# Moving a convolution's norm behind the last attention pair, and regrouping the first head of a recurrent layer

## The chip, the cores and the metric

The kernel runs on one core of one Trainium2 chip. The metric is the device time of one execution in microseconds (us), median of several runs. Engines are named as in the profile: PE is TensorE (matmuls; PEld are its weight loads), DVE is VectorE, ACT is ScalarE, POOL is GpSimd, SP is SyncE, whose queue issues the loads and stores.

## The reference, cut to what matters

One inference step through two layers, for a prompt of 512 tokens and for 8 sample sequences of 4 tokens that share the parameters (544 token columns, two halves of 272). The model width is 1024.

```
layer 0:  h = rms(x, norm_0);  q, k, v, g_att, u_a, u_b, g_conv = split(h @ w_in_0)
          attention of 8 heads (block-sparse over 256-token blocks; two blocks: all of the causal part)
          u = u_a * sigmoid(u_b);  y = depthwise_conv31(u) + b
          y = silu(layernorm(y, ln_g, ln_b))            # the convolution's norm, over 512 channels
          x = x + concat(o_att * silu(g_att), y * silu(g_conv)) @ w_out_0
layer 1:  h = rms(x, norm_1);  q, f, i, g = split(h @ w_in_1), 8 heads of 128
          gated linear recurrence per head, rms per head, gate, output projection, residual
```

Sample sequences attend over 256 cached positions (two pages of keys, two of values each). All in fp32 accuracy.

## The kernel before, in words

Activations lie transposed: channels on partitions, 544 tokens along the free axis in two halves of 272. Every projection goes by output blocks of 128 channels. `wtile` (L127) loads one block of weights (512 KB, by SP), and splits it on ACT (L133) and DVE (L134) into two fp32r parts. `unit` (L137) makes one half of one output block: 24 matmuls of 128x272 (L142 to L144) into a PSUM bank of tag "g". There are three banks "g", two of tag "s" (scores), two of tag "t" (transposes and sums) and one "o" (attention output).

Layer 0 works on head pairs 0 to 3. `prepkq` and `prepvg` project a pair, `attend` (L478) computes its prompt attention in four row blocks of 128 queries: for each of two heads the scores (PE, L484 and L486, bank "s"), the row maximum (DVE, L493), exp (ACT, L496), reciprocal (DVE, L497), scaling (ACT, L498), transposes through a bank "t" (PE by way of L102, copied by ACT, L503), and the product with the values (PE, L508). The convolution's 31 taps run as 30 DVE instructions per channel block (`taps`, L379); those of blocks 2 and 3 stand right ahead of the change.

Then, in the order of the source: the convolution's norm (L539 to L564): for each half, DVE adds the four channel blocks (L544, L546), one all-ones matmul sums over channels (L548, bank "t"), DVE subtracts the mean from four blocks (L551), ACT squares them (L553), DVE adds the squares (L555), a second all-ones matmul sums them (L557, bank "t"), ACT takes the square root (L559) and DVE the reciprocal (L560). Behind it the attention of pair 3, and behind that the four gate blocks of the convolution: eight units (L569), each queued behind the first scores of pair 3, with a tanh (L572) and a product (L573). Then the norm is applied (L580, L581), passed through silu (L583, L584) and multiplied by the gate (L585); the sample attention (scores L606, values L645), with pages loaded into the eight buffers "kn", of which the norm's two sum tiles are two; and the output projection in two halves (L666), with layer 1's statistics (L673 to L681).

In layer 1, `proj` (L732) makes a head's four projections ("jobs": f, q, v and g) in groups; a group's weights are loaded together and its units run job by job, first half, then second half. In the first head the second half of h is not yet normalised, so each second-half unit is multiplied by `r1b` (L768). `scan` (L785) is the recurrence; its steps are interleaved with the next head's projections.

The order of each engine's queue is not written by hand: a planner makes it when the program is built. It goes by the order of emission as priority and by its own estimate of when inputs are ready. `tc.issue_after(x)` adds that what is emitted inside is queued behind x on its engine. At run time each engine takes its queue in order.

Of the kernel before, what the change touches and what calls it, by code (L numbers as in the profile page):

```python
# [14 lines left out]
ALU = mybir.AluOpType  # L15
# [51 lines left out]
def hybrid_step(ctx, tc, xt_in, cache_kt, cache_v, conv_in, hgrn_in, page_table, par_in, k_norm_0,  # L67
# [18 lines left out]
    def bank(tag, cols=512, dt=F32):  # L86
        return pp.tile([128, cols], dt, name=nm(tag), tag=tag, bufs={"g": 3, "s": 2, "t": 2, "o": 1}[tag])
# [90 lines left out]
    with tc.tile_pool(name="l0", bufs=1) as lp:  # L178
# [54 lines left out]
        def scaled(ps, hf, u):  # L233
            e = mk(lp, "rs" if u else "ct", [128, HALF], 2)
            V.tensor_tensor(e, ps, rbc[hf], op=ALU.mult)
            return e
# [140 lines left out]
        def taps(c):  # L377
            for j in range(1, 31):
                V.scalar_tensor_tensor(cy[c][:, :TP], up[c][:, j:j + TP], cw[:, c, j:j + 1], cy[c][:, :TP],  # L379
                                       op0=ALU.mult, op1=ALU.add)  # L380
            G.tensor_scalar(up[c][:, 512:542], up[c][:, 512:542], 0.5, 0.0, op0=ALU.mult, op1=ALU.add)
            SP.dma_start(convp_out[:, c], up[c][:, 512:542])
# [93 lines left out]
            return c, rq, qT, kT, vt, ga  # L476

        def attend(c, rq, qT, kT, vt, ga):  # L478
            po, first = bank("o"), None
            for i in range(4):  # L480
                L = 128 * (i + 1)
                ss = [bank("s"), bank("s")]
                for hh in range(2):
                    sc = PE.matmul(ss[hh][:, :L], qT[:, i * 128:(i + 1) * 128], kT[:, hh, 0:L], start=True, stop=False)  # L484
                for hh in range(2):
                    PE.matmul(ss[hh][:, L - 128:L], identb, causb, start=False, stop=True)  # L486
                first = first or sc
                PTs = []
                for hh in range(2):
                    rqc = rq[:, 2 * i + hh:2 * i + hh + 1]  # L490
                    s = ss[hh]
                    mx = mk(lp, "mx", [128, 4], 4)
                    V.tensor_reduce(mx[:, 0:1], s[:, :L], axis=AX.X, op=ALU.max, negate=True)  # L493
                    A.activation(mx[:, 1:2], mx[:, 0:1], AF.Copy, scale=rqc)
                    P = mk(lp, "PP", [128, 512], 3)
                    A.activation(P[:, :L], s[:, :L], AF.Exp, bias=mx[:, 1:2], scale=rqc, accum_out=mx[:, 2:3])  # L496
                    V.reciprocal(mx[:, 3:4], mx[:, 2:3])  # L497
                    A.activation(P[:, :L], P[:, :L], AF.Copy, scale=mx[:, 3:4])  # L498
                    pT = bank("t")
                    for j in range(i + 1):  # L500
                        transpose(pT[:, j * 128:(j + 1) * 128], P[:, j * 128:(j + 1) * 128], 128)
                    PT = mk(lp, "PT", [128, 512], 3)
                    A.activation(PT[:, :L], pT[:, :L], AF.Copy)  # L503
                    PTs.append(PT)
                for j in range(i + 1):
                    for hh in range(2):
                        r = slice(64 * hh, 64 * hh + 64)
                        PE.matmul(po[r, i * 128:(i + 1) * 128], vt[:, j, r],  # L508
                                  PTs[hh][:, j * 128:(j + 1) * 128], start=(j == 0), stop=(j == i),
                                  tile_position=(0, 64 * hh))  # L510
            mh, ml = mtile(("h", c)), mtile(("l", c))
            V.scalar_tensor_tensor(ga[:, :TP], po, 0.5, ga[:, :TP], op0=ALU.mult, op1=ALU.mult)
            split(mh[:, :TP], ml[:, :TP], ga[:, :TP])
            return first

        def convout():
            for i in range(2):
# [17 lines left out]
        p3 = prepvg(*p3)  # L535
        taps(2)
        taps(3)
        rss = []
        at_ = [mk(lp, "kn", [128, T], 8) for _ in range(2)]  # L539
        accs = [[t[:, HC[hf]] for hf in range(2)] for t in at_]  # L540
        for hf in range(2):
            hs = HC[hf]
            acc = accs[0][hf]
            V.tensor_tensor(acc, cy[0][:, hs], cy[1][:, hs], op=ALU.add)  # L544
            for c in range(2, 4):
                V.tensor_tensor(acc, acc, cy[c][:, hs], op=ALU.add)  # L546
            pm = bank("t", HALF)
            PE.matmul(pm, ones, acc, start=True, stop=True)  # L548
            acc = accs[1][hf]
            for c in range(4):  # L550
                V.scalar_tensor_tensor(cy[c][:, hs], pm, -1.0 / 512, cy[c][:, hs], op0=ALU.mult, op1=ALU.add)  # L551
                sq = mk(lp, "ct", [128, HALF], 2) if c else acc
                A.activation(sq, cy[c][:, hs], AF.Square)  # L553
                if c:
                    V.tensor_tensor(acc, acc, sq, op=ALU.add)  # L555
            pq = bank("t", HALF)
            PE.matmul(pq, ones, acc, start=True, stop=True)  # L557
            rs = mk(lp, "rs", [128, HALF], 2)
            A.activation(rs, pq, AF.Sqrt, scale=1.0 / 512, bias=eps)  # L559
            V.reciprocal(rs, rs)  # L560
            rss.append(rs)
        pin = attend(*p3)
        gc = []
        for c in range(4):  # L564
            w = wtile(w_in_0, 3072 + c * 128)
            g2 = up[c]
            for hf in range(2):
                with tc.issue_after(pin.ins):
                    ps = unit(w, h, hf)  # L569
                ps = scaled(ps, 1, 0) if hf else ps  # L570
                tg = mk(lp, "tb", [128, HALF], 3)
                A.activation(tg, ps, AF.Tanh, scale=0.5)  # L572
                V.scalar_tensor_tensor(g2[:, HC[hf]], tg, 1.0, ps, op0=ALU.add, op1=ALU.mult)  # L573
            gc.append(g2)

        for c in range(4):
            tgs = []
            for hf in range(2):
# [107 lines left out]
    with tc.tile_pool(name="l1", bufs=1) as lp:  # L686
# [45 lines left out]
        def proj(hd):  # L732
            f, kk, qq = mk(lp, "f", [128, T], 2), mk(lp, "kk", [128, T], 2), mk(lp, "qq", [128, TP], 2)
            gg, vT = mtile(("gg", hd), F32), mtile(("vT", hd), F32)

            def ep_f(ps, hs):
                A.activation(f[:, hs], ps, AF.Sigmoid)  # L737

            qx = mk(lp, "qx", [128, T // 32, 80], 2)

            def ep_q(ps, hs):
                sg = mk(lp, "sg", [128, HALF], 4)
                A.activation(sg, ps, AF.Sigmoid)
                o = hs.start
                for a, b in ((0, 256), (256, 272)) if o == 0 else ((0, 16), (16, 272)):
                    n = max(1, (b - a) // 32)
                    t0 = (o + a) % 32
                    i0 = (o + a) // 32
                    V.tensor_tensor(qx[:, i0:i0 + n, t0:t0 + (b - a) // n], sg[:, a:b].rearrange("p (n t) -> p n t", n=n),
                                    ps[:, a:b].rearrange("p (n t) -> p n t", n=n), op=ALU.mult)  # L750

            def ep_g(ps, hs):
                sg = mk(lp, "sg", [128, HALF], 4)
                A.activation(sg, ps, AF.Sigmoid)
                V.tensor_tensor(gg[:, hs], sg, ps, op=ALU.mult)

            def ep_v(ps, hs):
                A.activation(vT[:, hs], ps, AF.Copy)

            jobs = ((1024, ep_f), (0, ep_q), (2048, ep_v), (3072, ep_g))  # L760
            for grp in (jobs[:2], jobs[2:]) if hd else ((jobs[2], jobs[0], jobs[1]), jobs[3:]):
                ws = [wtile(w_in_1, col + hd * 128) for col, _ in grp]
                for hf in range(2):
                    for w, (_, ep) in zip(ws, grp):
                        ps = unit(w, h, hf)
                        if hd == 0 and hf:
                            raw = mk(lp, "sg", [128, HALF], 4)
                            V.tensor_tensor(raw, ps, r1b, op=ALU.mult)  # L768
                            ps = raw
                        ep(ps, HC[hf])  # L770
            if hd == 0:
                normed(lp, "n1", r1b, 1)
            V.tensor_scalar(f, f, lbm[:, 5, hd:hd + 1], lbm[:, 4, hd:hd + 1], op0=ALU.mult, op1=ALU.add)
            G.tensor_scalar(kk, f, -1.0, 1.0, op0=ALU.mult, op1=ALU.add)
            vt = mk(lp, "vt", [128, 512], 2)
            pv = bank("t")
            for i in range(4):
                transpose(pv[:, i * 128:(i + 1) * 128], vT[:, i * 128:(i + 1) * 128], 128)
            A.activation(vt, pv, AF.Copy)
            vs = VS[hd % 2]  # L780
            vx = mk(lp, "vx", [128, 128], 2, F32R)
            rep4(vx, vT, (32, 96), 32, vs)
            return f, kk, qx, qq, vt, vs, vx, gg
# [291 lines left out]
```

## Time and profile before

| | |
|---|---|
| median of 3 runs | 661.8 us (661.76 to 663.45) |
| the profiled execution, its own time | 663.44 us |
| its span, first to last instruction | 661.6 us |
| PE busy | 631.2 us (95%) |
| DVE busy | 515.9 us (78%) |
| ACT busy | 367.6 us (56%) |
| POOL busy | 63.7 us (10%) |
| HBM traffic | 105 GB/s over the span |

Times in the profile are counted from the span's start. Busy time of PE is modelled from pipelined matmuls; idle time of PE between two matmuls is time in which none was in flight. The profiled execution was the slowest of the three; what lies around its span is 1.84 us.

### The profile page before, as it was taken

The numbers are of one execution on the slowest core, as the hardware profiler recorded it, in microseconds if no ns is written. First come the engines' busy times: TensorE is split into PE (matmuls) and PEld (weight loads), VectorE is DVE, ScalarE is ACT, GpSimd is POOL, SyncE is SP. The second block draws the span as 40 slices with busy tenths as digits, with TensorE's granted clock in tenths as the row PEclk, the third lists the DMA queues.
The fourth block names the chain that finished last, engine by engine and source line by source line (L and its number), as shares of the span: only waits on it lengthen the run. The fifth ranks groups of instructions, "written<-read, shape, count | busy, mean of one in ns | idle before, by whom it ended". The sixth has DMA issues, their size and how long they took to land.

```text
span 661.6 us, 14877 instructions
## 1 busy us (share of the span) xinstructions
PE 631.2 (95%) x5806; PEld 584.6 (88%) x5806; DVE 515.9 (78%) x1252; ACT 367.6 (56%) x908; POOL 63.7 (10%) x91
## 2 busy tenths in 40 slices
PE   8799999999999959989999899999999999999997
PEld 7699998998996848759999899998999999999997
DVE  6999898888989783846968887787777777776656
ACT  7334486387378475634747463737373737356421
POOL 6100000000100000000001311111111010121000
PEclk9799999999999969989999989999999999999999
DMA  9444321322431231774534134231414141322114
GB/s 297 116 85 108 113 75 41 91 73 64 97 82 65 85 125 33 246 265 149 167 109 158 34 92 135 67 130 38 154 41 143 55 135 62 116 78 92 46 57 148
DMA packets 39016, 70.58 MB, mean 107 GB/s; under 512 B 11938, under 2 KB 20642, under 8 KB 38946
## 3 DMA queue, kind: packets, MB, share of 16 engines
q1 hardware_dynamic: 38946, 69.63, 34.1%
q8 instruction: 46, 0.75, 0.5%
q14 instruction: 24, 0.20, 0.1%
HBM read 59.88 MB, written 9.73 MB: 105 GB/s over the span
## 4 chain that ended last, share of the span: by engine, by line
PE 81%; DVE 8%; ACT 5%; DMA 3%; issue 2%; SPq 1%; DVEq 0%; ACTq 0%
PE g L142 21%; PE g L144 20%; PE g L143 20%; PE t L102 4%; PE o L508 2%; PE s L484 2%; DVE wl L134 2%; ACT wh L133 1%; DMA kn<-in_cache_kt_dram 1%; PE t L933 1%; PE o L946 1%; DMA wr<-in_w_in_dram 1%; PE s L847 1%; PE o L948 1%; DVE tb L167 1%
## 5 line engine op out<-in xcount | busy, mean ns | idle before, releaser
L142 PE MATMUL g<-h,wh 128*128 128x272 f32 x944 | 279.2, 297 | 6.3 <-ACT f L737 3.1
L143 PE MATMUL g<-h,wh 128*128 128x272 f32 x944 | 277.3, 294 | 2.1 <-DVE h L273 2.1
L144 PE MATMUL g<-h,wl 128*128 128x272 f32 x944 | 277.6, 295 | 0.5 <-DVE wl L134 0.5
L142 PEld LDWEIGHTS g<-h,wh 128*128 128x128 f32 x944 | 180.1, 191 | 11.3 <-ACT f L737 3.6
L143 PEld LDWEIGHTS g<-h,wh 128*128 128x128 f32 x944 | 180.0, 191 | 4.8 <-DVE h L273 2.7
L144 PEld LDWEIGHTS g<-h,wl 128*128 128x128 f32 x944 | 180.2, 191 | 3.4 <-issue 2.0
L133 ACT ACTIVATE wh<-wr 128x1024 fp32r<-128x1024 f32 (+4 forms) x90 | 88.0, 980 | 94.2 <-PE g L143 91.3
L134 DVE TENSOR_TENSOR wl<-wr,wh 128x1024 fp32r<-128x1024 f32 (+4 forms) x90 | 101.5, 1129 | 15.0 <-ACT wh L133 14.8
L379 DVE SCALAR_TENSOR_TENSOR m<-m,vecs,m 128x512 f32<-128x512 f32 x120 | 87.4, 740 | 0.7
L142 PE MATMUL g<-m,wh 128*128 128x272 f32 x256 | 75.1, 297 | 0.0
L144 PE MATMUL g<-m,wl 128*128 128x272 f32 x256 | 74.3, 292 | 0.0
L143 PE MATMUL g<-m,wh 128*128 128x272 f32 x240 | 70.0, 293 | 0.0
L142 PEld LDWEIGHTS g<-m,wh 128*128 128x128 f32 x256 | 48.5, 191 | 3.9 <-issue 2.7
L144 PEld LDWEIGHTS g<-m,wl 128*128 128x128 f32 x256 | 48.8, 191 | 1.2 <-issue 1.0
L143 PEld LDWEIGHTS g<-m,wh 128*128 128x128 f32 x240 | 45.8, 191 | 0.1
L910 DVE TENSOR_TENSOR qq<-qq,tot 128x256 f32<-128x256 f32 x24 | 10.0, 415 | 24.9 <-ACT kv L875 22.4
L484 PE MATMUL s<-kz,qT 128*128 128x128 f32 (+3 forms) x64 | 22.8, 447 | 1.4 <-ACT PP L496 1.3
L503 ACT ACTIVATE PT<-t 128x128 f32<-128x128 f32 (+3 forms) x32 | 13.8, 432 | 16.3 <-PE t L102 16.3
L955 POOL TENSOR_TENSOR ve<-vx,cst 128x1024 fp32r<-128x1024 f32 x8 | 15.4, 1930 | 77.1 <-DVE vx L730 63.6
L953 ACT ACTIVATE S<-S,tot 128x128 f32<-128x128 f32 x64 | 20.4, 390 | 1.6 <-PE t L852 1.5
L1014 DVE TENSOR_TENSOR xTall<-g,xTall 128x272 f32<-128x272 f32 x32 | 13.5, 436 | 8.8 <-PE g L144 8.3
L874 ACT ACTIVATE kv<-kk 128x256 f32<-128x256 f32 x16 | 6.6, 411 | 24.5 <-DVE kk L911 20.5
(299 smaller groups left out, 1027.1 us busy)
## 6 DMA issues: line engine op xcount, KB each, us to landing
wr<-in_w_in_dram SPq DMA_DIRECT2D x58, 512.0 KB, 3.7
wr<-in_w_out_dram SPq DMA_DIRECT2D x16, 512.0 KB, 3.6
kn<-in_cache_kt_dram SPq DMA_DIRECT2D x16, 256.0 KB, 4.0
kn<-in_cache_v_dram SPq DMA_DIRECT2D x16, 256.0 KB, 4.4
S<-in_hgrn_dram SPq DMA_DIRECT2D x8, 512.0 KB, 3.6
out_hgrns_dram<-S SPq DMA_DIRECT2D x8, 512.0 KB, 2.6
xTall<-in_xt_dram SPq DMA_DIRECT2D x8, 272.0 KB, 5.5
out_y_dram<-xTall SPq DMA_DIRECT2D x8, 272.0 KB, 2.9
```

What stands on the lines that cost most here:

```text
L102: PE.transpose(out, in_, ident[:np_, :np_])
L133: A.activation(wh, raw, AF.Copy)
L134: V.tensor_tensor(wl, raw, wh, op=ALU.subtract)
L142: PE.matmul(ps, wh[:, k - k0, :], ah, start=(k == k0), stop=False)
L143: PE.matmul(ps, wh[:, k - k0, :], al, start=False, stop=False)
L144: PE.matmul(ps, wl[:, k - k0, :], ah, start=False, stop=(k == k1 - 1))
L379: V.scalar_tensor_tensor(cy[c][:, :TP], up[c][:, j:j + TP], cw[:, c, j:j + 1], cy[c][:, :TP], op0=ALU.mult, op1=ALU.add)
L484: sc = PE.matmul(ss[hh][:, :L], qT[:, i * 128:(i + 1) * 128], kT[:, hh, 0:L], start=True, stop=False)
L503: A.activation(PT[:, :L], pT[:, :L], AF.Copy)
L953: A.activation(S0[:, n], S0[:, n], AF.Copy, scale=tots[:, n:n + 1])
L955: G.tensor_tensor(ve, vx.unsqueeze(1).to_broadcast([128, NS, 128]), exm.unsqueeze(2).to_broadcast([128, NS, 128]), op=ALU.mult)
L1014: V.tensor_tensor(xT[c][:, HC[hf]], ps, xT[c][:, HC[hf]], op=ALU.add)
```

## The change

`attend` returns the last scores matmul of each of its four row blocks instead of that of the first one. The attention of pair 3 is emitted ahead of the norm; so are the gate blocks 0 and 1 (`gates(0)`, `gates(1)`), still queued behind the first row block's scores. Then comes the norm, with two differences: its four sums go to banks "g" instead of "t", and the sum of squares of half 0 is queued behind the third row block's scores, that of half 1 behind the fourth's. `gates(2)` and `gates(3)` follow the norm. In layer 1 the first head's jobs come in the groups (f, q) and (v, g), as in all other heads, instead of (v, f, q) and (g). No arithmetic is added or taken away.

```diff
--- before.py
+++ after.py
@@ -476,7 +476,7 @@
             return c, rq, qT, kT, vt, ga
 
         def attend(c, rq, qT, kT, vt, ga):
-            po, first = bank("o"), None
+            po, firsts = bank("o"), []
             for i in range(4):
                 L = 128 * (i + 1)
                 ss = [bank("s"), bank("s")]
@@ -484,7 +484,7 @@
                     sc = PE.matmul(ss[hh][:, :L], qT[:, i * 128:(i + 1) * 128], kT[:, hh, 0:L], start=True, stop=False)
                 for hh in range(2):
                     PE.matmul(ss[hh][:, L - 128:L], identb, causb, start=False, stop=True)
-                first = first or sc
+                firsts.append(sc)
                 PTs = []
                 for hh in range(2):
                     rqc = rq[:, 2 * i + hh:2 * i + hh + 1]
@@ -511,7 +511,7 @@
             mh, ml = mtile(("h", c)), mtile(("l", c))
             V.scalar_tensor_tensor(ga[:, :TP], po, 0.5, ga[:, :TP], op0=ALU.mult, op1=ALU.mult)
             split(mh[:, :TP], ml[:, :TP], ga[:, :TP])
-            return first
+            return firsts
 
         def convout():
             for i in range(2):
@@ -535,6 +535,23 @@
         p3 = prepvg(*p3)
         taps(2)
         taps(3)
+        pins = attend(*p3)
+        gc = []
+
+        def gates(c):
+            w = wtile(w_in_0, 3072 + c * 128)
+            g2 = up[c]
+            for hf in range(2):
+                with tc.issue_after(pins[0].ins):
+                    ps = unit(w, h, hf)
+                ps = scaled(ps, 1, 0) if hf else ps
+                tg = mk(lp, "tb", [128, HALF], 3)
+                A.activation(tg, ps, AF.Tanh, scale=0.5)
+                V.scalar_tensor_tensor(g2[:, HC[hf]], tg, 1.0, ps, op0=ALU.add, op1=ALU.mult)
+            gc.append(g2)
+
+        gates(0)
+        gates(1)
         rss = []
         at_ = [mk(lp, "kn", [128, T], 8) for _ in range(2)]
         accs = [[t[:, HC[hf]] for hf in range(2)] for t in at_]
@@ -544,7 +561,7 @@
             V.tensor_tensor(acc, cy[0][:, hs], cy[1][:, hs], op=ALU.add)
             for c in range(2, 4):
                 V.tensor_tensor(acc, acc, cy[c][:, hs], op=ALU.add)
-            pm = bank("t", HALF)
+            pm = bank("g", HALF)
             PE.matmul(pm, ones, acc, start=True, stop=True)
             acc = accs[1][hf]
             for c in range(4):
@@ -553,26 +570,15 @@
                 A.activation(sq, cy[c][:, hs], AF.Square)
                 if c:
                     V.tensor_tensor(acc, acc, sq, op=ALU.add)
-            pq = bank("t", HALF)
-            PE.matmul(pq, ones, acc, start=True, stop=True)
+            pq = bank("g", HALF)
+            with tc.issue_after(pins[2 + hf].ins):
+                PE.matmul(pq, ones, acc, start=True, stop=True)
             rs = mk(lp, "rs", [128, HALF], 2)
             A.activation(rs, pq, AF.Sqrt, scale=1.0 / 512, bias=eps)
             V.reciprocal(rs, rs)
             rss.append(rs)
-        pin = attend(*p3)
-        gc = []
-        for c in range(4):
-            w = wtile(w_in_0, 3072 + c * 128)
-            g2 = up[c]
-            for hf in range(2):
-                with tc.issue_after(pin.ins):
-                    ps = unit(w, h, hf)
-                ps = scaled(ps, 1, 0) if hf else ps
-                tg = mk(lp, "tb", [128, HALF], 3)
-                A.activation(tg, ps, AF.Tanh, scale=0.5)
-                V.scalar_tensor_tensor(g2[:, HC[hf]], tg, 1.0, ps, op0=ALU.add, op1=ALU.mult)
-            gc.append(g2)
-
+        gates(2)
+        gates(3)
         for c in range(4):
             tgs = []
             for hf in range(2):
@@ -758,7 +764,7 @@
                 A.activation(vT[:, hs], ps, AF.Copy)
 
             jobs = ((1024, ep_f), (0, ep_q), (2048, ep_v), (3072, ep_g))
-            for grp in (jobs[:2], jobs[2:]) if hd else ((jobs[2], jobs[0], jobs[1]), jobs[3:]):
+            for grp in (jobs[:2], jobs[2:]):
                 ws = [wtile(w_in_1, col + hd * 128) for col, _ in grp]
                 for hf in range(2):
                     for w, (_, ep) in zip(ws, grp):
```

## Rows read from the trace of the kernel before

**Rows 1.** Page, second part: granted TensorE clock in 40 slices, tenths of full.

```profile
PEclk9799999999999969989999989999999999999999
```

**Rows 2.** Waits of TensorE, whole run: us in total, times, longest us.

```profile
PE t L557 <- DVE kn L555: 8.2, 1, 8.2
PE g L142 <- ACT f L737: 3.1, 2, 2.1
...
PE s L645 <- DMA kn<-in_cache_v_dram: 2.1, 1, 2.1
```

**Rows 3.** Timeline, TensorE: start us, duration us, engine, line, op, tiles, count, idle.

```profile
222.38 0.86 PE L484 MATMUL s<-kz,qT 128*128 128x384 f32 x2
...
223.45 0.29 PE L142 MATMUL g<-h,wh 128*128 128x272 f32 x1
...
225.19 0.29 PE L144 MATMUL g<-h,wl 128*128 128x272 f32 x1
...
231.02 0.62 PE L557 MATMUL t<-kn,ones 128*128 128x272 f32 x2
231.48 0.62 PE L548 MATMUL t<-kn,ones 128*128 128x272 f32 x2
240.29 1.27 PE L557 MATMUL t<-kn,ones 128*128 128x272 f32 x2 [8.19 <-DVE kn L555]
...
241.80 0.43 PE L143 MATMUL g<-h,wh 128*128 128x272 f32 x1
...
245.43 0.36 PE L144 MATMUL g<-h,wl 128*128 128x272 f32 x1
...
253.35 1.02 PE L484 MATMUL s<-kz,qT 128*128 128x512 f32 x2
```

**Rows 4.** Windows: stretch, its length; busy us (instructions) per engine; clock; DMA share.

```profile
232.00:240.00 8.00, 0.10 (x1) 0.00 (x0) 7.86 (x17) 4.59 (x8) 0.00 (x0) 0.71 0.60 208
240.00:246.00 6.00, 5.71 (x24) 5.37 (x25) 4.31 (x9) 5.08 (x10) 0.00 (x0) 0.54 0.13 44
246.00:262.00 16.00, 16.00 (x114) 12.52 (x113) 7.71 (x20) 10.67 (x26) 0.00 (x0) 1.00 0.11 34
290.00:294.00 4.00, 4.00 (x21) 3.44 (x18) 0.44 (x1) 0.00 (x0) 0.00 (x0) 0.58 1.00 381
347.00:361.00 14.00, 12.96 (x104) 12.96 (x105) 12.01 (x30) 11.06 (x18) 2.11 (x9) 1.00 0.59 195
```

**Rows 5.** Timeline, VectorE, 232 to 241 us.

```profile
232.14 1.48 DVE L551 SCALAR_TENSOR_TENSOR m<-t,m 128x272 f32<-128x272 f32 x4 [2.34 <-PE t L548]
...
234.67 1.84 DVE L560 RECIPROCAL rs<-rs 128x272 f32<-128x272 f32 x1
...
239.81 0.43 DVE L555 TENSOR_TENSOR kn<-kn,ct 128x272 f32<-128x272 f32 x1
```

**Rows 6.** Timeline, ScalarE, 241 to 246 us.

```profile
241.67 1.28 ACT L559 ACT_TABLE_LOAD   x1
242.97 0.49 ACT L559 ACTIVATE rs<-t,eps 128x272 f32<-128x272 f32 x1
...
243.64 1.28 ACT L496 ACT_TABLE_LOAD   x1
244.93 0.56 ACT L496 ACTIVATE PP<-s,mx,rq 128x256 f32<-128x256 f32 x1
```

**Rows 7.** Timeline, TensorE, the end of the third pair's attention.

```profile
210.61 0.49 PE L484 MATMUL s<-kz,qT 128*128 128x128 f32 x2 [0.64 <-ACT PP L496]
...
212.28 0.49 PE L484 MATMUL s<-kz,qT 128*128 128x128 f32 x2 [0.63 <-ACT PP L496]
```

**Rows 8.** Timeline, ScalarE, where layer 1 begins.

```profile
340.33 0.40 ACT L758 ACTIVATE m<-g 128x272 f32<-128x272 f32 x1 [2.15 <-PE g L144]
...
345.79 0.49 ACT L680 ACTIVATE r1b<-t,eps 128x272 f32<-128x272 f32 x1 [3.80 <-PE t L679]
...
347.59 0.40 ACT L737 ACTIVATE f<-g 128x272 f32<-128x272 f32 x1
```

## The prediction

> **What bounds the kernel now.** I read the page's first two parts, then the waits of TensorE, then the timeline of each engine around the longest of them. TensorE has work nearly all the time, so only what stops it, or halves its clock, is worth moving. The slices of the granted clock show where that is: full speed but for the start and three dips, the deepest in slice 15 of 40 (232 to 248 us at 16.5 us a slice) [rows 1]. The waits name the cause: one wait of 8.2 us at L557, the second matmul of the convolution's norm, for the squares that VectorE adds up; everything else that stops TensorE is 3.1 us in two pieces or less per line [rows 2].
>
> The timeline shows what the reader should see there [rows 3]. The sum of half 0 (L557) runs at 231.02, the mean of half 1 (L548) at 231.48, and the next thing in TensorE's queue is L557 of half 1, which starts at 240.29. Queues are taken in order, so behind it stood the remaining attention of pair 3 and the gate blocks. In those 8 us VectorE was busy 7.86 of 8.00 [rows 4]: it waited for the mean (2.34 us), subtracted it, took a reciprocal of 1.84 us for half 0, scaled half 0 and ended its last addition at 240.24 [rows 5]. The attention stood still too: scores of the third row block had run at 222.38, those of the fourth came at 253.35 [rows 3]. An exp of the second row block, whose scores are older still, ran at 244.93, behind the square root of half 1 and two table loads [rows 6].
>
> **The change, part by part.**
>
> *The norm behind the attention.* No instruction is added. What goes is the 8.19 us for which TensorE stood at L557 [rows 3]. With it goes the slow clock behind it: it is 0.71 in the 8 us and 0.54 in the 6 us after [rows 4], that is the lower level, 1.2 GHz. At full clock 14 steps from 223.45 to 225.19 take 0.124 us each; at the lower one 16 steps from 241.80 to 245.43 take 0.227 us each [rows 3]. That is 16 x 0.103 = 1.64 us. The pair of L557 took 1.07 us to the next instruction at 241.36 against 0.46 (231.02 to 231.48), 0.61 more; the edges add about 0.1. Sum 2.4 us. So the stall is worth 8.2 + 2.4 = 10.6 us.
>
> What covers it now? From 222 us on TensorE has the rest of pair 3's attention, what is left of gate blocks 0 and 1, which ran from 223 to 231 (some 7.5 us) [rows 3], and blocks 2 and 3, four units of 24 matmuls, 11.9 us at 0.124, all independent of the norm. With attention first on VectorE and ScalarE, the third and fourth blocks' softmax run while VectorE adds squares, and a wait at a sum has other work ahead of it. VectorE can carry this: from 232 to 262 it was busy 7.86 + 4.31 + 7.71 = 19.9 us of 30 [rows 4], and the same work in 10.6 us less would be 19.9 in 19.4. That would be full if all of it had to fall there, but the scaling by the reciprocals (L580, L581) is not wanted before the silu chain, so what is late next, if anything, is that chain and not TensorE.
>
> *Two sums behind row blocks.* The waits added are on TensorE's own order. Queued behind a sum that is late are the gate units and transposes; who waits for them is ScalarE, which copies. The mean (L548) is not pinned; behind VectorE's L551, which waits for it, stand row maxima of the attention. Bounds: nothing, up to the 2.34 us of [rows 5] for each half. I take it with the next item, since both show as waits inside the attention.
>
> *The banks.* The sums leave the two "t" banks to the attention's transposes and hold one of three "g" banks: the mean's through four L551, 1.48 us [rows 5], the squares' until a square root. A gate unit may wait for one. Bounds 0 to 1.5 us a sum.
>
> *Square roots between exps.* Each square root sits between two table loads of 1.28 us: 1.28 + 0.49 + 1.28 = 3.05 us in which ScalarE makes no exp [rows 6]. Before, they fell while the attention stood still; now they fall into it. Two of them cost 6.1 us if nothing covers them, 0 if gate units do. The nearest rows are the third pair's attention, with square roots of its own in front and VectorE full: TensorE waited 0.64 and 0.63 us there for exps [rows 7]. I take their sum, 1.3 us, for this, the sums and the banks together.
>
> The Trainium skill ("ScalarE: Activation LUTs", What ACT_TABLE_LOAD costs) puts a switch at about 1283 ns for the load and about 1380 ns more for a drain, 2.66 us in all. The trace has the load, 1.28 us, and no such drain: the load of 243.64 ends at 244.92 and the exp starts at 244.93 [rows 6]. By the Trainium skill's figure the uncovered price of the two square roots would be 2 x (5.32 + 0.49) = 11.6 us instead of 6.1, which would eat the whole gain; the trace decides for 6.1.
>
> *Loads.* The norm's two sum tiles are buffers of "kn", so the last of the first eight loads of cached keys waits for the second sum as it did; SP's queue behind it holds weights. The gate weights of blocks 2 and 3 are now emitted behind the norm and could stand behind that load. Their matmuls come some 10 us later than the load is due. I cost it at 0; if that cover goes, a wait like VectorE's for a sum, 2.3 us [rows 5], is the other end.
>
> *First head in (f, q), (v, g).* Before, TensorE ran the first halves of v, f, q and the second of v, and then waited for a bank: the two waits for L737 are 3.1 us, the longer 2.1 [rows 2], so this one is 1.0. The bank was f's, whose sigmoid at 347.59 stood in ScalarE's queue behind the square root of `r1b` at 345.79, for which ScalarE had idled 3.80 us [rows 8]. Now f is the first unit; the first unit ended at 340.33 (there v's copy starts), so its sigmoid and q's can run in that idle time and give their banks back before a fourth unit needs one. In return `r1b` comes one table load (1.28 us) later and two second-half units wait for it instead of one; the third bank lets v go on. Bounds: 1.0 us gained to 1.3 lost; I take the gain, 1.0. f is also complete earlier, but VectorE is busy 12.01 of 14 us behind it [rows 4] with the normalisation and the first scan, so I take 0 for that, with 3.8 us as the other end (below).
>
> **The sum.** 8.2 + 2.4 + 1.0 - 1.3 = 10.3 us. The profiled execution took 663.44 us, span 661.6 and 1.84 around it, and two of the three runs lie at 661.8, so the saving is taken from the median: 661.8 - 10.3 = 651.5 us.
>
> **The rivals.**
>
> *More comes back.* The other wait for L737, 2.1 us [rows 2], lies behind the first head. After the wait for cached values, as long [rows 2], the clock was 0.58 over 4 us [rows 4]: 3.4 us at the lower level, half of them lost, 1.7 us. If the wait behind the first head costs the same, 3.8 us, f's earlier end clears it, and the attention needs no 1.3, it is 651.5 - 5.1 = 646.4 us. For it: the idle ScalarE before 345.79. Against: VectorE's load. Chance 0.14.
>
> *Part is given back.* The planner interleaves by its own estimates; if it knows nothing of the table loads, TensorE meets both square roots at a transpose: 6.1 instead of 1.3 us, 656.3 us. For it: the order before was wrong by 8 us at just this place. Against: some 150 gate matmuls can stand in between. Chance 0.17.
>
> *It doesn't do what it says.* The pin fixes only that a sum comes after a row block's scores, not that work stands ahead of it. If VectorE's squares still end at 240 and the planner again puts the second sum first, the wait stays and only the 1.0 us is gained: 660.8 us. Against: the priority is now the other way round. Chance 0.06.
>
> *Slower.* Five softmax chains of pair 3 are left at 222 us (one of the second row block, two each of the third and fourth). If TensorE stands 2.1 us at each of four for ScalarE, and each time falls to the lower clock (1.7 us), it costs 4 x 3.8 = 15.2 us against the 11.6 gained (8.2 + 2.4 + 1.0): 665.4 us. It decides from the third such wait (11.4). For it: ScalarE held by 3.05 us twice. Against: in the third pair's attention no wait was over 0.64 [rows 7]. Chance 0.05.
>
> **How the numbers follow.** The forecast, 651.5, has 0.58, alone from 648 to 655. 0.3% of 661.8 is 2 us, about what a measurement here can tell from no change. Faster is the forecast, "more" and "part" less a tail of 0.02 beyond 659.8: 0.87. Within 2 us is that tail and "doesn't do": 0.08. Slower 0.05. The range reaches into "more" and over "part": 645.5 to 657.5.
>
> **What would show it.** In the changed kernel's trace: no wait over 2.5 us at the norm's sums, and clock 1.00 from 222 to 260; scores of the fourth row block near 230 to 240 instead of 253; the last gate unit, the sample scores and the output projection some 10 us earlier; ScalarE's sigmoid of f ahead of the square root of `r1b`, and no wait of TensorE there. It is wrong if the wait stands at another sum or transpose, if the silu chain behind the norm ends no earlier than before, so that the output projection waits for it, or if the first head loses what the norm gains.

## The result and the profile after

The changed kernel takes 655.4 us (median of 4 runs, 654.8 to 656.5) against 661.8 us for the kernel before on the same chip; the ratio is 0.9906, 95% interval 0.9889 to 0.9922. That is 6.4 us less. The forecast was 651.5 us in a range of 645.5 to 657.5: the sign and the range held, the size did not, 6.4 us for the 10.3 forecast. The nearest rival by number is "part is given back" (656.3), but not by the mechanism that it named.

The profiled execution of the changed kernel has a span of 652.9 us and a time of 655.62 us. The first view is its granted clock in 40 slices (16.3 us each).

```profile
PEclk9799999999999997999999999999999999999999
```

Of the three dips in [rows 1] one is left, in slice 16 (245 to 261 us). The waits of TensorE say what stands there now (us in total, times, longest).

```profile
PE s L612 <- DMA kn<-in_cache_kt_dram: 6.0, 3, 3.0
...
PE g L142 <- ACT f L743: 2.7, 1, 2.7
...
PE t L102 <- ACT PP L498: 1.1, 1, 1.1
```

The 8.2 us at the norm's second sum [rows 2] is gone. In its place stand 6.0 us for cached keys at the sample scores (L612) and 1.1 us at a transpose. In the kernel before, the scores (there L606) had waited 0.9:

```profile
PE s L606 <- DMA kn<-in_cache_kt_dram: 0.9, 1, 0.9
```

TensorE's timeline gives the order in the changed kernel.

```profile
231.76 1.02 PE L484 MATMUL s<-kz,qT 128*128 128x512 f32 x2
...
235.43 1.02 PE L484 MATMUL s<-kz,qT 128*128 128x512 f32 x2
...
236.34 0.68 PE L565 MATMUL g<-kn,ones 128*128 128x272 f32 x2
...
241.47 0.66 PE L102 MATMUL t<-cst,PP 128*128 128x128 f32 x4 [1.13 <-ACT PP L498]
242.26 0.73 PE L575 MATMUL g<-kn,ones 128*128 128x272 f32 x2
...
245.55 1.08 PE L612 MATMUL s<-kn,qbd 128*32 128x128 f32 x32 [1.08 <-DMA kn<-in_cache_kt_dram]
249.62 1.62 PE L612 MATMUL s<-kn,qbd 128*32 128x128 f32 x32 [2.99 <-DMA kn<-in_cache_kt_dram]
...
253.88 1.94 PE L612 MATMUL s<-kn,qbd 128*32 128x128 f32 x32 [1.91 <-DMA kn<-in_cache_kt_dram]
255.75 1.24 PE L575 MATMUL g<-kn,ones 128*128 128x272 f32 x2
```

The attention now runs through: the fourth row block's scores are at 231.76 and 235.43, where one of them came at 253.35 in [rows 3]. Neither sum of squares (L575: 242.26 and 255.75) waits, since the second stands behind three groups of sample scores that do. 1.13 + 1.08 + 2.99 + 1.91 = 7.1 us of TensorE's time goes there. The windows (columns as in [rows 4]) show the price in the clock.

```profile
240.00:246.00 6.00, 3.65 (x40) 2.49 (x44) 3.70 (x8) 4.74 (x10) 0.00 (x0) 1.00 0.96 349
246.00:256.00 10.00, 5.10 (x122) 3.79 (x115) 7.06 (x19) 4.54 (x7) 0.00 (x0) 0.70 0.70 227
256.00:262.00 6.00, 6.00 (x44) 5.77 (x45) 4.42 (x9) 2.17 (x3) 0.00 (x0) 0.93 0.67 220
```

From 246 to 256 us TensorE is busy 5.10 of 10 us at 0.70. Between full speed and the lower level that is 2 x 0.30 x 10 = 6.0 us at 1.2 GHz, and 0.8 us more in the next window; before it was 2 x 0.29 x 8 + 2 x 0.46 x 6 = 10.2 us in the two windows of [rows 4]. So the hole is shallower, not closed. (The slices hide a shorter stretch, 0.88 from 342 to 356 us, behind the wait for f.)

Why does TensorE wait for keys that were in time before? It asks for them earlier: the sample scores begin at 245.55, where they began at 264.59 before. And the loads start later. SyncE's queue: first the changed kernel, then the kernel before (start, duration, queue, line, tile, count).

```profile
227.52 11.21 SPq L130 DMA_DIRECT2D wr<-in_w_out_dram  x2
239.00 7.97 SPq L606 DMA_DIRECT2D kn<-in_cache_kt_dram  x8
```

```profile
226.99 0.35 SPq L130 DMA_DIRECT2D wr<-in_w_out_dram  x1
227.60 4.87 SPq L600 DMA_DIRECT2D kn<-in_cache_kt_dram  x7
234.78 0.34 SPq L130 DMA_DIRECT2D wr<-in_w_out_dram  x1
```

Before, seven key loads were issued from 227.60 on, and the next weight load came behind them at 234.78. Now a second weight load stands ahead of the keys: it is the second of the first row, issued at 238.39, as soon as VectorE has ended the split that frees its buffer. It is one of the output projection; the last gate weights were issued by 190 us in both kernels. The first key load follows at 239.00, 11.4 us later than before. VectorE's row of that split:

```profile
237.15 1.22 DVE L134 TENSOR_TENSOR wl<-wr,wh 128x1024 fp32r<-128x1024 f32 x1
```

That delay is in the first of the three waits only. Each group of scores needs four keys, and by the trace the last key of each group landed at 245.50, 249.57 and 253.84 us, some 0.05 us ahead of the scores. The fourth load (issued at 240.66) cost 1.08 us. The eighth went out at 246.64 only, when the first scores had been read and a buffer was free, since the norm's second tile still held one of the eight "kn": 2.99 us. The twelfth went out at 251.23, again behind scores that freed a buffer: 1.91 us.

For the stages I put four marks on TensorE: the last sum of squares of the pairs' q and k, the first projection of layer 1, and the first scan products (L847, L841 before) of layer 1's second and eighth head. The times between them, worked out from the traces:

```
us               start   layer 0's rest   first head   heads 2 to 8   end     span
before          191.65       142.51         60.07         204.71     62.64   661.58
after           192.17       137.87         60.61         201.37     60.90   652.92
after, again    191.71       139.02         59.13         201.31     60.88   652.05
old first head  192.23       136.95         61.16         203.00     60.78   654.12
regroup alone   192.76       140.87         60.66         201.32     60.78   656.38
(v, q, f)       191.55       141.78         59.15         202.16     60.79   655.42
all three       191.29       135.90         60.04         200.92     60.79   648.94
gates ahead     191.68       144.35         61.83         201.37     60.79   660.02
```

Half of the gain is not where it was forecast: layer 0's rest gives 4.6 us, heads 2 to 8 and the end give 3.3 + 1.7 = 5.1, and the first head loses 0.5. (The profiled executions lie 7.8 us apart, 8.7 by their spans, since that of before is 1.7 above its median.)

The marks inside layer 1 part different work in the two kernels: ahead of the second head's mark TensorE is busy 56.0 us before and 58.0 after, behind it 260.5 and 258.5. So layer 1 is best read as a whole: 327.4 us before, 322.9 after, busy 316.6 and 316.5. All but 0.1 of its gain of 4.5 us is idle time. The wait for f in the first head grows by 1.6 (1.06 to 2.65); gone are the three waits shown next, 3.0 us, 2.3 us at L933 in the later heads (shown below), and 0.7 us behind the last matmul.

```profile
371.59 0.36 PE L142 MATMUL g<-h,wh 128*128 128x272 f32 x1 [0.46 <-DVE qx L749]
...
380.21 0.39 PE L142 MATMUL g<-h,wh 128*128 128x272 f32 x1 [2.06 <-ACT f L737]
...
381.19 0.39 PE L144 MATMUL g<-h,wl 128*128 128x272 f32 x1 [0.46 <-DVE wl L134]
```

### The profile page after: what moved, and what is told of

Its sections match the earlier page's. It is cut to its first block, busy times and chain, and to the rows that moved or that the text cites. A ratio compares the mean times of both kernels' runs of the same rounds, so it can differ in the third digit from the quotient of the medians.

```text
span 652.9 us, 14858 instructions
## 1 busy us (share of the span) xinstructions
PE 629.5 (96%) x5806; PEld 581.9 (89%) x5806; DVE 524.8 (80%) x1252; ACT 365.5 (56%) x908; POOL 62.7 (10%) x91
## 4 chain that ended last, share of the span: by engine, by line
PE 88%; DVE 4%; DMA 3%; ACT 3%; SPq 1%; issue 1%; DVEq 0%; ACTq 0%
PE g L142 23%; PE g L143 23%; PE g L144 22%; PE t L102 5%; PE s L484 2%; PE o L508 2%; DMA kn<-in_cache_kt_dram 2%; PE o L952 1%; PE t L939 1%; PE s L847 1%; DMA kn<-in_cache_v_dram 1%; PE s L612 1%; PE s L853 1%; DMA xTall<-in_xt_dram 1%; PE o L954 1%
## 5 line engine op out<-in xcount | busy, mean ns | idle before, releaser
L143 PE MATMUL g<-h,wh 128*128 128x272 f32 x944 | 277.9, 295 | 1.9 <-DVE h L273 1.7
L143 PEld LDWEIGHTS g<-h,wh 128*128 128x128 f32 x944 | 179.6, 190 | 6.0 <-DVE h L273 3.1
L133 ACT ACTIVATE wh<-wr 128x1024 fp32r<-128x1024 f32 (+4 forms) x90 | 88.1, 981 | 91.1 <-PE g L143 84.5
L142 PE MATMUL g<-m,wh 128*128 128x272 f32 x256 | 74.0, 293 | 0.3 <-ACT wh L133 0.3
L143 PE MATMUL g<-m,wh 128*128 128x272 f32 x240 | 69.6, 290 | 0.0
L143 PEld LDWEIGHTS g<-m,wh 128*128 128x128 f32 x240 | 45.2, 188 | 1.1 <-DVE ct L590 0.8
L959 ACT ACTIVATE S<-S,tot 128x128 f32<-128x128 f32 x64 | 20.5, 390 | 11.4 <-PE t L858 11.4
L916 DVE TENSOR_TENSOR qq<-qq,tot 128x256 f32<-128x256 f32 x24 | 11.7, 486 | 14.8 <-PE s L888 12.0
L917 DVE TENSOR_TENSOR kk<-kk,tot 128x256 f32<-128x256 f32 (+1 forms) x48 | 20.0, 417 | 0.3
```

What stands on the lines that cost most here:

```text
L133: A.activation(wh, raw, AF.Copy)
L142: PE.matmul(ps, wh[:, k - k0, :], ah, start=(k == k0), stop=False)
L143: PE.matmul(ps, wh[:, k - k0, :], al, start=False, stop=False)
L917: V.tensor_tensor(k3[:, :, 0, :], k3[:, :, 0, :], t3[:, :, 1:2].to_broadcast([128, nblk, hsz]), op=ALU.mult)
L959: A.activation(S0[:, n], S0[:, n], AF.Copy, scale=tots[:, n:n + 1])
```

## The experiments

Ratios are to the kernel before, run on the same chip: its median was 662.3 us beside e1 to e4, 663.4 beside e5 to e8 and 662.3 beside e9 to e11. Each diff is against the changed kernel unless it says otherwise. The theory at the outset: the norm's gain is cut because the sums' banks hold the last gate blocks back and the keys are loaded late, so both can be had back. Its rival: the waits only move. For the later heads: the groups of two gain there, or any other order does.

**Which half gave what.** e3 keeps the first head's old groups, e4 makes the regroup alone in the kernel before.

```diff
 # e3
-            for grp in (jobs[:2], jobs[2:]):
+            for grp in (jobs[:2], jobs[2:]) if hd else ((jobs[2], jobs[0], jobs[1]), jobs[3:]):
```

> The changed kernel with layer 1's first head in the groups of before, (v, f, q) and (g). Layer 1 is 4.5 us shorter in the changed kernel (322.9 instead of 327.4 us from its first matmul to the end), though its first wait for a bank is longer (2.65 instead of 1.06 us). Theory H (the regrouping shortens layer 1 by what comes after that wait): time 4 to 5 us longer than the changed kernel's, about 660 us. Rival J (the regrouping only costs: 1.6 us at the first wait; the rest of layer 1 is shorter because layer 0 ends otherwise): 1 to 2 us shorter, about 654 us.

> The kernel before with only the first head regrouped. Theory H: layer 1 is about 4.5 us shorter, time about 657 us. Rival J: 662 to 664 us.

e3 took 657.6 us, 0.9932 [0.9911, 0.9954]; e4 658.1 us, 0.9914 [0.9883, 0.9946]. Alone the norm gives some 0.7% and the regroup some 0.9%, together 0.9%: they do not add. e4 came out as the regrouping theory had it, e3 half-way between the two. The waits of TensorE in e3 and then in e4:

```profile
PE g L142 <- ACT f L743: 3.1, 2, 2.1
```

```profile
PE t L557 <- DVE kn L555: 8.2, 1, 8.2
...
PE g L142 <- ACT f L737: 2.6, 1, 2.6
```

So the regrouping is what clears the second wait for f (2.06 us, kept in e3) and what lengthens the first. e4 keeps the whole 8.2 us wait at the norm and still gains 5.3 us in heads 2 to 8 and at the end (stage table), 4.7 over all of layer 1. The kernel before has waits there that no other has; this is its whole list from 400 to 600 us, which is empty in the changed kernel, e3, e4 and e8:

```profile
PE t L933 <- ACT ktk L927: 2.3, 4, 0.6
```

**Is it the groups of two?** e8 makes another order in the kernel before: still three jobs, with f last.

```diff
-... if hd else ((jobs[2], jobs[0], jobs[1]), jobs[3:]):
+... if hd else ((jobs[2], jobs[1], jobs[0]), jobs[3:]):
```

> The kernel before with the first head still in a group of three and one, but in the order (v, q, f) and (g). Rival P (the later heads and the end are shorter not for the groups of two but because any change there makes the planner settle in another repeating order; the regrouped kernel before and the changed kernel with the old groups both have it): from the second head on 4 to 5 us shorter than before, as in both; time 656 to 660 us. Theory H (the groups of two do it): as before, 661 to 664 us.

e8 took 657.9 us, 0.9933 [0.9903, 0.9963]. Its heads 2 to 8 and end take 202.16 + 60.79 = 262.95 us, against 267.35 before and 262.27 after; all of layer 1 takes 322.1, against 327.4 and 322.9. So groups of two are not needed. e3, e4 and e8 touch different places and all leave the order with the four waits; from head to head the spacing falls from 33.64 to 33.28 us. The four waits belong to the order in which the planner settled, and each of these edits tips it. The gain at the end is weaker evidence: 0.7 of its 1.7 us lie behind the last matmul, and e6, with the same TensorE time there, has 1.8 us more (62.60 us in all).

**The first head itself.** In the changed kernel TensorE waits 2.65 us at 342.26 for f; before, 1.06 at 348.04. ScalarE's timeline there:

```profile
339.07 1.06 ACT L133 ACTIVATE wh<-wr 128x1024 fp32r<-128x1024 f32 x1 [3.14 <-PE g L143]
340.03 0.47 ACT L686 ACTIVATE r1b<-t,eps 128x272 f32<-128x272 f32 x1
340.52 1.28 ACT L743 ACT_TABLE_LOAD   x1
```

The sigmoid of f still stands behind `r1b`'s square root (L686), and behind a weight split (L133) that idles 3.14 us for a matmul. e6 moves both behind q's sigmoid.

```diff
-            A.activation(r1s[hf], pr_, AF.Sqrt, scale=1.0 / D, bias=eps)
 ...
+                    with (tc.issue_after(sig[1].ins) if hd == 0 and col == 3072 else nullcontext()):
+                        ws.append(wtile(w_in_1, col + hd * 128))
 ...
+                    if hd == 0 and hf and grp is first:
+                        A.activation(r1b, pr_, AF.Sqrt, scale=1.0 / D, bias=eps)
```

> The changed kernel with two moves at the start of layer 1: the square root and reciprocal of the second half's statistics are emitted behind the first head's two first units, and the weights of g are split behind the sigmoid of q. Theory E (the 2.65 us wait of TensorE for a bank is ScalarE's queue: the split of g's weights waits 3.1 us for TensorE, and f's sigmoid stands behind it and the square root): the wait goes, with its low clock (0.88 over 14 us) 3 to 4 us, time 651 to 653 us. Rival F (it turns into a wait for r1b, which now comes a table load later, or for the split of g): a wait of 1.5 us or more stays before 350 us, time 654 to 657 us.

e6 took 655.7 us, 0.9883 [0.9840, 0.9925]: alone no change that can be told, as the rival had it. In e6, TensorE's row of a sum and ScalarE's timeline:

```profile
339.92 0.62 PE L685 MATMUL t<-tb,ones 128*128 128x272 f32 x2
```

```profile
340.62 1.28 ACT L743 ACT_TABLE_LOAD   x1 [3.76 <-PE t L685]
```

The wait fell to 1.8 us only. No square root and no split stands before the sigmoid now, and ScalarE still idles 3.76 us until the second half's sum for layer 1's norm (L685) is through at 340.54, though f's first unit had long ended. By its arithmetic f needs nothing of this sum. f's tile is taken from layer 1's pool (`mk(lp, "f", ...)`), and the first tiles written there by VectorE (lbm) and GpSimd (AD) are released by the same sum; v's copy, which the kernel before had first, writes a tile from outside that pool and ran at 340.33 [rows 8], ahead of the sum. So the likely cause is that layer 1's pool takes over layer 0's memory and that this sum is among the last to read it; no run tests it.

**The norm's banks and tiles.** e1 gives the sums the banks of the transposes again, e2 takes the two norm tiles out of "kn" (from the tag "kr", which the head pairs have done with), e5 does both.

```diff
 # e1
-            pm = bank("g", HALF)
+            pm = bank("t", HALF)
 ...
-            pq = bank("g", HALF)
+            pq = bank("t", HALF)
 # e2
-        at_ = [mk(lp, "kn", [128, T], 8) for _ in range(2)]
+        at_ = [mk(lp, "kr", [128, T], 2) for _ in range(2)]
```

> The changed kernel with the norm's four sums back in banks t; nothing else differs. Theory A (the sums in banks g hold the gate blocks 2 and 3 behind the last sum, because buffers of one tag are handed out in the order of emission): the 96 gate matmuls spread over the fourth row block and the sums, the four waits between 240 and 256 us (1.1 + 1.1 + 3.0 + 1.9 = 7.1 us) nearly go, time about 648 to 650 us. Theory B (the cached keys are loaded too late, from 239 instead of 227 us, since the norm's tiles stand ahead of them among the buffers kn): the scores of the samples wait as before, time 654 to 656 us.

> The changed kernel with the norm's two sum tiles in the buffers kr, which are dead by then, instead of kn; so the cached keys no longer queue behind them. Theory A: the gate blocks stay behind the last sum, TensorE stands for that sum instead of the keys; of the 7.1 us of waits at most half goes, time 652 to 655 us. Theory B: the keys land by 235 us, the 7.1 us go, time 648 to 650 us.

> The changed kernel with both edits of the first two experiments: the norm's sums in banks t and its two sum tiles in the dead buffers kr. Theory C (two things hold TensorE after the change and either is enough: the gate blocks stay behind the last sum, and the cached keys come late; taking away one leaves the other): the four waits of 7.1 us between 240 and 256 go down to at most 1.5 us, no low clock there, time 647 to 650 us. Rival D (the work between 220 and 260 is bound by VectorE and ScalarE, and a wait moves to wherever TensorE next needs them): waits of 5 us or more stay somewhere between 235 and 290 us, time 653 to 656 us.

They took 654.2 us (0.9867 [0.9844, 0.9889]), 655.7 us (0.9887 [0.9869, 0.9904]) and 654.6 us (0.9876 [0.9840, 0.9911]). All three intervals overlap the changed kernel's of its second set of runs (0.9871 to 0.9927), e1's only touches that of the first (0.9889 to 0.9922); by the medians they are 1.2 us under it to 0.3 above. None reached the 647 to 650 us of the theory that it was to test. The timelines of TensorE at the new waits, in e1, e2 and e5:

```profile
259.11 1.08 PE L612 MATMUL s<-kn,qbd 128*32 128x128 f32 x32 [2.60 <-DMA kn<-in_cache_kt_dram]
...
264.76 1.93 PE L612 MATMUL s<-kn,qbd 128*32 128x128 f32 x32 [4.07 <-DMA kn<-in_cache_kt_dram]
```

```profile
246.89 1.08 PE L612 MATMUL s<-kn,qbd 128*32 128x128 f32 x32 [0.77 <-DMA kn<-in_cache_kt_dram]
...
251.90 1.50 PE L612 MATMUL s<-kn,qbd 128*32 128x128 f32 x32 [1.71 <-DMA kn<-in_cache_kt_dram]
...
255.82 1.93 PE L651 MATMUL s<-kn,PT 128*32 128x512 f32 x8 [1.69 <-DMA kn<-in_cache_v_dram]
```

```profile
259.86 0.73 PE L575 MATMUL t<-kr,ones 128*128 128x272 f32 x2 [1.95 <-DVE kr L572]
262.79 1.93 PE L612 MATMUL s<-kn,qbd 128*32 128x128 f32 x32 [2.21 <-DMA kn<-in_cache_kt_dram]
```

Each edit does what it was to do. In e1 gate matmuls fill the stretch (32 of line L143 run from 236 to 256 us, none in the changed kernel). In e2 the first eight keys are loaded long ahead, six from 20 us on and the last at 186.79, and their scores run from 238.39 without a wait:

```profile
20.07 6.22 SPq L606 DMA_DIRECT2D kn<-in_cache_kt_dram  x6
...
186.79 0.35 SPq L606 DMA_DIRECT2D kn<-in_cache_kt_dram  x1
...
241.17 5.34 SPq L606 DMA_DIRECT2D kn<-in_cache_kt_dram  x8
```

```profile
238.39 0.43 PE L612 MATMUL s<-kn,qbd 128*32 128x128 f32 x8
```

But the waits move on. In e1 the key loads pause from 241.9 to 254.8 us, until the second mean (L565 at 254.12) gives back the norm's first tile. In e2 TensorE waits for the second eight keys, which need the buffers of the first eight (241.17), and for values, and the gates are still behind the second sum. In e5 the cover is spent when the last square arrives, and the second keys come later still (from 256.54). Idle in layer 0's rest is 8.6, 8.9 and 9.3 us, against 9.6 in the changed kernel and 12.6 before.

**Gates ahead of everything.** e11 emits all four gate blocks ahead of the norm, with e2's tiles and the sums in banks "g".

```diff
-        gates(0)
-        gates(1)
+        for c in range(4):
+            gates(c)
 ...
-        gates(2)
-        gates(3)
```

> All four gate blocks emitted ahead of the norm (so the order in which the banks g are handed out can't hold blocks 2 and 3 behind the sums), sums still in banks g, the norm's two tiles from a tag of their own. Theory A (the order of emission within the tag g held the gate blocks): the last gate unit ends before 262 us instead of 268.7, key loads begin near 228 us, waits in the attention fall to 2 to 4 us in all; 653 to 654.5 us. Theory B (the blocks came last for their pins or their place in the planner's estimates, not for the banks): gate units still behind the second square sum, 655 to 656 us.

e11 took 659.9 us, 0.9965 [0.9944, 0.9985], slower than the changed kernel by 4 us where both theories had it at 653 to 656. The mechanism of theory A is there, mirrored: the first sum of the norm runs at 253.25, behind all gate units, where it ran at 236.34. Emission order in the tag "g" decides which comes last. What A had wrong is the worth of it. TensorE in e11, timeline and windows:

```profile
253.25 0.62 PE L565 MATMUL g<-kr,ones 128*128 128x272 f32 x2
...
258.55 1.06 PE L575 MATMUL g<-kr,ones 128*128 128x272 f32 x2 [2.28 <-DVE kr L572]
...
264.56 1.08 PE L610 MATMUL s<-kn,qbd 128*32 128x128 f32 x32 [1.45 <-DMA kn<-in_cache_kt_dram]
...
269.58 1.93 PE L649 MATMUL s<-kn,PT 128*32 128x512 f32 x8 [2.38 <-DMA kn<-in_cache_v_dram]
```

```profile
246.00:256.00 10.00, 10.00 (x153) 9.09 (x155) 6.27 (x12) 4.43 (x8) 0.00 (x0) 1.00 0.19 55
256.00:262.00 6.00, 3.46 (x60) 2.10 (x48) 4.67 (x10) 3.08 (x6) 0.00 (x0) 0.73 0.93 290
262.00:270.00 8.00, 4.17 (x90) 2.17 (x86) 6.72 (x21) 5.49 (x11) 0.00 (x0) 0.93 0.95 314
```

TensorE is full to 256 us and then has nothing to put beside the norm, the second keys and the values: 2.54 + 3.83 = 6.4 us idle in 14 us. The first eight keys were there, as in e2; the next load went out at 254.90, when their scores, at 253.81, began to give buffers back. Layer 0's rest is longer than in the kernel before (stage table).

**All three, and the changed kernel again.** e7 and e10 are e5 and e6 together; e9 is the changed kernel.

> The norm's sums in banks t, its tiles in kr, and the two moves at the start of layer 1. Theories C and E together: 643 to 647 us. If only C holds, 647 to 650; if only E, 651 to 653.

> The changed kernel once more, beside the two kernels below on one chip, to compare them directly. Theory A (the norm's gain is cut by the key loads and by the gate blocks that come last): as before, 654.5 to 656.5 us, the waits for cached keys of some 6 us in all and one of 2.7 us for f in layer 1. Theory B (the differences between these versions are what the chip varies by): it comes out within 1 us of the next kernel.

> Sums in the transposes' banks, the norm's two tiles from a pool tag of their own, and r1b's square root behind f's sigmoid. Theory A: 652 to 653.5 us, 2 to 3 us under the changed kernel on the same chip, no wait for cached keys over 2.5 us before the sample scores, wait for f 1.8 us. Theory B: within 1 us of the changed kernel.

e7 took 652.6 us, 0.9853 [0.9819, 0.9887], far from the 643 to 647 of both theories. On one chip e9 took 655.7 us (654.5 to 656.9, 6 runs), 0.9899 [0.9871, 0.9927], and e10 652.7 us (650.7 to 653.2, 5 runs), 0.9844 [0.9814, 0.9874]. The two sets of runs do not overlap: this version beats both kernels, by 3.0 us the changed one. Its gain is not one wait: keys 2.1 instead of 6.3 us, f 1.8 instead of 2.6, and 1.9 new at the norm's sum.

## Why the prediction held in sign and missed in size

**The stall (8.2 + 2.4 us): mechanism right, worth half.** The wait at the norm's sum went. In the two profiles TensorE's idle time in layer 0's rest fell by 2.9 us only (12.6 to 9.6), its busy time, which holds what the clock costs, by 1.7 (130.0 to 128.2). The stretch of layer 0 gained 4.6 us in the profiles shown, and over all profiles with either norm 3.5: 142.51, 140.87 and 141.78, mean 141.7, against 137.87, 139.02, 136.95 and 138.87 (e6), mean 138.2. The forecast for it was 8.2 + 2.4 - 1.3 = 9.3.

**Loads at 0: the step that failed.** I saw that the eighth key load waits for a buffer that the norm holds, and put it at 0; the other end that I gave was 2.3 us. The keys cost 6.0, against 0.9 before. I reckoned with gate weights standing behind that load, but these had been loaded by 190 us. What stood in SyncE's queue was a weight load of the output projection, ahead of all keys, and it accounts for 1.1 of the 6.0; the other 4.9 are loads that had to wait for one of the eight buffers. Nor did I ask what the change itself moves forward: the sample scores want their keys 19 us earlier than before. Yet loads at the right time are not enough by themselves: e2 had the first eight keys in time and was no faster.

**The cover: half wrong.** I counted blocks 2 and 3, 11.9 us of matmuls, as work that could stand beside the norm. In the changed kernel no gate matmul ran from 236 to 256 us; e1 and e11 show that the order of emission within the banks "g" sets this. With them there (e1, e5) the medians moved by 0.8 to 1.2 us, which the intervals don't tell from nothing, since keys and squares then came late at another place. That the gate blocks' place alone explains the missing gain is therefore not so. What I take to be short is TensorE work for the stretch in which norm, keys and values all arrive: each edit chose which of them TensorE stands for. A rival is not tested: no run has more than eight buffers "kn", and in every run some loads of keys or values waited for one.

**Square roots between exps: near by luck.** 1.3 us was taken, and a transpose waited 1.13 us, but not for a square root. ScalarE's timeline:

```profile
238.50 0.77 ACT L496 ACTIVATE PP<-s,mx,rq 128x512 f32<-128x512 f32 x1
...
239.73 0.44 ACT L570 ACTIVATE kn<-m 128x272 f32<-128x272 f32 x1
240.05 0.75 ACT L570 ACTIVATE ct<-m 128x272 f32<-128x272 f32 x2
240.69 0.72 ACT L498 ACTIVATE PP<-PP,mx 128x512 f32<-128x512 f32 x1
...
242.78 1.28 ACT L577 ACT_TABLE_LOAD   x1
244.07 0.49 ACT L577 ACTIVATE rs<-g,eps 128x272 f32<-128x272 f32 x1
```

The transpose waited for the scaling at 240.69, which had three squares of the norm (L570) before it in the queue. The attention's last exp ran at 238.50, the first table load for a square root at 242.78. So none fell between exps, and the rival with 6.1 us by this cause did not occur. The Trainium skill has a drain of about 1380 ns on top of the load at each switch of table sets ("ScalarE: Activation LUTs", What ACT_TABLE_LOAD costs). It is not in this trace either: the load of 1.28 us ends at 244.06, and the square root starts at 244.07.

**First head (1.0 us gain): the wait went the wrong way, and a gain unforeseen.** The wait rose from 1.06 to 2.65 us, 1.6 lost where 1.3 was the worst that I had. I put f's and q's sigmoids "in that idle time" of 3.8 us, but f's can't run before the second half's sum (e6), and in the changed kernel a split and the square root stood before it as well. The stage as a whole is within what one execution varies by: 60.61 us in one profile, 59.13 in the other, with the same wait, against 60.07 before. What I put at 0 is the rest of layer 1. The second wait for f, which I had named under "more comes back", went, with two of 0.46 us beside it, and 2.3 us at L933 went in work that the edit does not touch. Why the kernel before alone settled in the order with L933's waits stays open.

**Two readings.** Of the third and fourth row blocks I took one head's scores for both: in the kernel before the other heads' ran at 246.84 and 250.33. And VectorE's 2.34 us for the mean lie ahead of the 8 us in which I counted them. No sum hangs on either.

That the total came within 4 us is in part luck. In the profiles layer 0 gave 4.7 us less than the 9.3 forecast, and layer 1 gave 3.5 more than the 1.0. Of the signs that I named, the scores at 230 to 240 us came true; the clock at 1.00 to 260 us and f ahead of `r1b`'s square root did not. The sample scores came 19 us earlier, but the last gate unit (268.70 for 264.37) and the output projection (270.77 for 268.14) came later.

## What to carry to other kernels

When a long wait goes, list everything that was due during or behind it, loads first: work that moves forward needs its loads, and the buffers for them, earlier than before, or the wait comes back under another name. Moving covering work forward only helps if something is left for the last arrival; e11 filled TensorE to 256 us and came out 4 us slower. A planner that interleaves by estimates can answer a small edit with another order in stages far away, so test each part alone before crediting it, and compare stages only where they hold the same work.

## What the runs showed of the hardware

Key loads of 256 KB that are issued within 5 us land one after the other: in e2 the eight issued from 241.17 to 246.18 us landed from 244.89 to 251.85. In the changed kernel the DMA share was 0.96 at 349 GB/s from 240 to 246 us, when the first keys came in. A VectorE reciprocal of 128x272 takes 1.84 us, an addition of the same shape 0.43 [rows 5]. TensorE's clock was still 1.00 from 240 to 246 us, over waits of 1.1 us each, and 0.70 from 246 to 256, where it was busy half of the time. The same wait for f of 2.65 us was followed by 0.88 over 14 us in one profile of the changed kernel (342 to 356 us) and by 1.00 in the other.
